# Paired score matmuls in a forgetting-attention mixer, and its convolution rows placed behind the weight splits on VectorE

## The chip, the cores and the metric

One core of a Trainium2 chip runs the whole program once. The time is device microseconds of one execution; smaller is better. Engines are called as in the profile: PE is TensorE's matmul side, PEld its weight load, DVE is VectorE, ACT is ScalarE, POOL is GpSimd, SP issues the DMAs.

## What is computed

A 256-token, 1024-wide float32 activation goes through three mixers and four feed-forward layers (FFN), in the order: differential attention with pooling, FFN 0, sliding-window attention, FFN 1, FFN 2, the forget mixer, FFN 3, final norm. The change matters in the forget mixer:

```
proj = rms_norm(x, mix_norm) @ w_in                 # a, g, q, k, v, fl
u = a * sigmoid(g)                                  # 512 channels
y = causal depthwise conv of u, 31 taps, + bias
y_conv = silu(layer_norm(y))
cum = cumsum(log_sigmoid(fl + forget_b))            # per head
s = q k^T / 8 + cum[query] - cum[key], causal       # 8 heads of 64, blocks of 128 queries
y_attn = softmax(s) v
x = x + concat(rms_norm(y_conv), rms_norm(y_attn)) @ w_out
```

The two attention mixers before it compute scores with the same helper.

## The kernel before, in words

**Tiling.** Tokens are two blocks of 128 (`tb` 0 and 1). Each weight matrix comes as tiles of 128 x 2048 float32 (1 MB). A tile is loaded by an SP DMA into one of two staging tiles `st`, then split in two: ACT casts it to the rounded part `whi` (two pieces of 128x1024, line 218) and DVE subtracts to get the rest `wlo` (four pieces of 128x512, line 222). `whi` and `wlo` have five buffers each. Each product is three matmuls, of lines 271, 272, 273 or 521, 522, 523: `whi` with the activation's rounded part, `wlo` with it, `whi` with the activation's rest. So PE needs both parts of a weight, a new cast needs the buffer of the fifth cast before it, and a new DMA needs a staging tile that has been read by ACT and DVE.

**Order.** The program is written in one order, and a scheduler in the build orders each engine's instructions by readiness and priority. Work under `tc.high_priority(offset=-N)` is set N places later in priority. The splits stand under `-LATER` (400) and the convolution's rows under `-LATERC` (300), so both give way to the work of the moment. Once built, each engine runs its own list in order and waits at an instruction whose input or buffer isn't ready.

**The forget mixer.** `conv_in(j)` projects 128 channels of a and g into `ag`; `cv[j].gate()` makes `u` from them (`th` on ACT, `u` on DVE). `conv_rows(cv[j])` adds the taps: each row is one DVE instruction over up to 256 tokens, `ys<-u,dwh,ys` (line 1090); tap 30 is the last, 226 tokens wide. One of the four channel blocks has 11 of its taps on PE (`cv`, line 1105). `proj_qk(s, b)` projects block b of q (s = 0) or k (s = 1) with 24 matmuls into `qk`; ACT copies it out. A block holds two heads, in partitions 0 to 63 and 64 to 127. `f0` and `f1` are the attention of the two query blocks; `scores(*blks)` calls `softmax_rows` (line 632: the q k product `sc<-qk,qk`, 64 rows deep, written in two passes and so two matmuls in the trace; lines 1158 and 1160: the gates' matmuls added into the same PSUM tile; line 635: DVE's reading of the tile, `S`, with the row minimum `nm`), then the exponentials on ACT. `ptp` and `o` are transposes and values; `on` (line 911) is the normed attention output, `z` (line 1178) its gated norm, `pt` the transposes of a `z`, and `mixT` the result, rounded part by ACT (line 289) and rest by DVE (line 290).

**The end of the mixer.** `conv_norm(tb)` transposes the convolution's `ys` on PE (`yT`, line 1192), takes mean and variance (BN_STATS), and goes through `yc`, `th` (ACT), `yc`, the square sum `junk` (ACT, line 299), `ss` (DVE), a power on POOL, `z`, `pt`, `mixT`. The output projection `op` has four weight tiles: two for the attention half of `mixT` (48 matmuls of 512 columns for both token blocks), two for the convolution half (48 more). Then come the residual, a norm and `lead`, the first matmuls of FFN 3.

Of the kernel before, what the change touches and what calls it, by code (L numbers as in the profile page):

```python
# [14 lines left out]
ALU = mybir.AluOpType  # L15
# [4 lines left out]
S = 256  # L20
# [8 lines left out]
SLOPES_A = [2.0 ** (-8.0 * (i + 1) / 4) for i in range(4)]  # L29
SLOPES_C = [float(np.float32(2.0) ** np.float32(-8.0 * (i + 1) / 16)) for i in range(16)]  # L30
# [5 lines left out]
FIRST = {("w0", 0): 4, ("w0", 1): 2}  # L36
TB, UB = 6, 5
NPE = (0, 11, 0, 0)
LATERC = 300
VCOPY = {((1, 0), 4), ((0, 0), 4), ((0, 1), 2), ((1, 1), 0), ((1, 1), 6)}  # L40
O_PS = {(1, 0), (1, 1)}
DENG = "AAAA"
# [67 lines left out]
def block_kernel(ctx: ExitStack, tc: tile.TileContext, a: dict, out: bass.AP):  # L110
    nc = tc.nc
    V, A, T, G = nc.vector, nc.scalar, nc.tensor, nc.gpsimd
# [12 lines left out]
    def ps_t(name="ps"):  # L125
        return pps.tile([P, 512], F32, tag="ps", name=name)

    def t512(name="t512"):
        return tmp.tile([P, 512], F32, tag="t512", name=name, bufs=TB)

    def b4(dt=F32, name="b4"):
        return tmp.tile([P, 1024], dt, tag="b4", name=name, bufs=5)
# [18 lines left out]
    def C(n, i=0, w=None):  # L151
        o, full = CC[n]
        return cc[:, o + i:o + i + (full - i if w is None else w)]
# [121 lines left out]
    def cut(pair, *idx):  # L275
        return tuple(t[idx] for t in pair)

    def tok(tb):
        return slice(tb * P, (tb + 1) * P)
# [98 lines left out]
    def v3(pair, k):  # L378
        return tuple(t.rearrange("p (k n) -> p k n", k=k) for t in pair)
# [139 lines left out]
    def mm_w(o, w, xT, ko, first, last):  # L519
        x = cut(xT, slice(None), ko, slice(0, S))  # L520
        T.matmul(o, w[0], x[0], start=first, stop=False)
        T.matmul(o, w[0], x[1], start=False, stop=False)
        T.matmul(o, w[1], x[0], start=False, stop=last)
# [56 lines left out]
    kTA = b4(name="kTA").rearrange("p (b t) -> p b t", b=4)  # L580
    qTA = b4(name="qTA").rearrange("p (b t) -> p b t", b=4)
# [38 lines left out]
        A.activation((qTA, kTA)[s][:, :, tok(tb)], transposes(hn.pop((s, tb)), 4).rearrange("p (b t) -> p b t", b=4),  # L620
                     AF.Copy, scale=(nqg, PVs("kg"))[s])

    def softmax_rows(qT, kT, heads, tb, rel, nm, den, SP, extra=None):

        L = P * (tb + 1)
        per = 512 // L
        for i in range(0, len(heads), per):
            pst = ps_t("sc")
            Sx = t512("S")
            for n, (r0, qb, kb, slope, idx) in enumerate(heads[i:i + per]):  # L630
                o = pst[:, n * L:(n + 1) * L]
                T.matmul(o, qT[r0:r0 + 64, qb, :], kT[r0:r0 + 64, kb, 0:L], start=True, stop=extra is None)  # L632
                if extra is not None:
                    extra(o, idx, L)
                V.tensor_tensor_reduce(Sx[:, n * L:(n + 1) * L], o, rel[:, S - L:S], slope, 3e38,
                                       ALU.add, ALU.min, nm[:, idx:idx + 1])
                SP[idx] = Sx[:, n * L:(n + 1) * L]

    def exps(idxs, SP, nm, den):
        for idx in idxs:  # L640
            A.activation(SP[idx], SP[idx], AF.Exp, bias=nm[:, idx:idx + 1], scale=-1.0,
                         accum_out=den[:, idx:idx + 1])

    class AttendA:
# [4 lines left out]

        def scores(self, *hs):  # L650
            tb, SP, rd, den = self.tb, self.SP, self.rd, self.den
            for m in range(2):
                softmax_rows(qTA[:, :, tok(tb)], kTA, [(64 * m, h, h, SLOPES_A[h], 2 * h + m) for h in hs],
                             tb, C("rel"), self.nm, den, SP)
            exps([2 * h + m for m in range(2) for h in hs], SP, self.nm, den)
            i = slice(2 * hs[0], 2 * hs[-1] + 2)
            V.reciprocal(rd[:, i], den[:, i])
            two = lambda t: t[:, i].rearrange("p (h m) -> p h m", m=2)
            ra = self.ra[:, hs[0]:hs[-1] + 1]
            V.scalar_tensor_tensor(ra, two(rd)[:, :, 1], nlam, two(den)[:, :, 0], ALU.mult, ALU.mult)  # L660
            for h in hs:
                p0, p1 = SP[2 * h], SP[2 * h + 1]
                V.scalar_tensor_tensor(p0, p1, self.ra[:, h:h + 1], p0, ALU.mult, ALU.add)
# [169 lines left out]
    qTC = [b4(name="qTC").rearrange("p (b t) -> p b t", b=4) for _ in range(2)]  # L833
# [81 lines left out]
    class AttendC(Values):  # L915
# [4 lines left out]
        def scores(self, *blks):  # L920
            c, tb, SP, nm, den, sk = self.c, self.tb, self.SP, self.nm, self.den, self.sk
            kT1 = kTC[c].rearrange("p (o t) -> p o t", o=1)
            for e in range(2):
                softmax_rows(qTC[c][:, :, tok(tb)], kT1,
                             [(64 * e, b, 0, SLOPES_C[8 * c + 2 * b + e], 2 * b + e) for b in blks],
                             tb, C("relw"), nm, den, SP)
            i = slice(2 * blks[0], 2 * blks[-1] + 2)
            V.tensor_tensor(nm[:, i], nm[:, i], nsink[:, 8 * c:8 * c + 8][:, i], ALU.min)
            exps([2 * b + e for e in range(2) for b in blks], SP, nm, den)
            V.tensor_tensor(sk[:, i], nm[:, i], srow[:, 8 + 8 * c:16 + 8 * c][:, i], ALU.add)  # L930
            A.activation(sk[:, i], sk[:, i], AF.Exp)
            V.tensor_tensor(den[:, i], den[:, i], sk[:, i], ALU.add)
            V.reciprocal(self.rd[:, i], den[:, i])
# [103 lines left out]
    for h in range(2):  # L1037
        hs = slice(h * 512, (h + 1) * 512)
# [17 lines left out]
    def conv_in(j):  # L1056
        ag[j] = ps_t("ag").rearrange("p (s t) -> p s t", s=2)
        w = v3(W.get("w2", j), KD)
        for s in range(2):
            for ko in range(KD):  # L1060
                mm_w(ag[j][:, s, :], cut(w, slice(None), ko, slice(s * P, (s + 1) * P)),
                     xT, ko, ko == 0, ko == KD - 1)
        W.free(("w2", j))
# [70 lines left out]
    def conv_rows(c):  # L1134
        with tc.high_priority(offset=-LATERC):
            c.rows()
# [4 lines left out]
    q2, k2 = (b4(name=f"qk{s}").rearrange("p (b t) -> p b t", b=4) for s in range(2))  # L1141

    def proj_qk(s, b):
        o = ps_t("qk")
        for ko in range(KD):
            mm_w(o[:, :S], cut(v3(W.get("w2", 4 + 2 * s + ko // 4), 4), slice(None), ko % 4, slice(b * P, (b + 1) * P)),
                 xT, ko, ko == 0, ko == KD - 1)
        A.activation((q2, k2)[s][:, b, :], o[:, :S], AF.Copy, scale=1.0 if s else -0.125)
        if b == 3:
            W.free(("w2", 4 + 2 * s), ("w2", 5 + 2 * s))  # L1150

    class AttendF(Values):
# [8 lines left out]
                         stop=kb == L // P - 1)  # L1161

        def scores(self, *blks):
            for e in range(2):
                softmax_rows(q2[:, :, tok(self.tb)], k2, [(64 * e, b, b, 1.0, 2 * b + e) for b in blks],
                             self.tb, C("mask"), self.nm, self.den, self.SP, self.gate)
            exps([2 * b + e for e in range(2) for b in blks], self.SP, self.nm, self.den)
            i = slice(2 * blks[0], 2 * blks[-1] + 2)
            V.reciprocal(self.rd[:, i], self.den[:, i])
# [37 lines left out]
    f0, f1 = AttendF(0), AttendF(1)  # L1207
    cv = [Conv(j, NPE[j]) for j in range(4)]
# [16 lines left out]
    proj_qk(0, 1)  # L1225
    conv_in(3)
    conv_rows(cv[2])
    proj_qk(1, 2)
    proj_qk(1, 1)
    proj_qk(0, 2)  # L1230
    proj_qk(1, 0)
    proj_qk(0, 3)
    cv[3].gate()
    f1.scores(0, 1)
    conv_rows(cv[3])
    f0.scores(0, 1)
    proj_qk(1, 3)
    f1.values_T(2, 3)
    f1.scores(2, 3)
# [133 lines left out]
```

## Time and profile before

| what | value |
| --- | --- |
| median of 3 runs | 1063.0 us |
| the runs shown | 1060.22, 1063.0, 4472.5 us |
| the profiled execution | 1060.59 us |
| its span in the trace | 1058.7 us |
| granted TensorE clock | 0.999 |
| PE, DVE, ACT busy | 1040.9, 779.4, 622.2 us |

The profiled execution is 1.9 us longer than its span and 2.4 us below the median of the runs shown. The forget mixer lies at about 745 to 865 us of the span. A busy share counts an engine as busy from the start to the modelled end of its instructions, so short steps in which matmuls follow each other slowly don't show as idle; there, the distance from one start to the next is what tells.

### The profile page before, as it was taken

To read this page: it belongs to the slowest core of one execution; us is meant where nothing else is said; L and a number is where in the kernel's file an instruction comes from. 1 tells how busy PE (TensorE), PEld (TensorE's weight loads), DVE (VectorE), ACT (ScalarE), POOL (GpSimd) and SP (SyncE) were. 2 spreads that over 40 slices of the span, in tenths; PEclk is the share of its full clock that TensorE was granted. 3 is DMA by queue.
4 is the path that set the end of the run, shared out by engine and by line. 5 is a ranking of instruction groups with operands and counts; after the bars stand their busy time and mean duration, and the time that the engine had idled before them with its cause. 6 is when DMAs were issued, how large, how long until landed. Compare 5 with 4: busy or idle time off the path is not lost.

```text
span 1058.7 us, 15504 instructions
## 1 busy us (share of the span) xinstructions
PE 1040.9 (98%) x5873; PEld 892.1 (84%) x5873; DVE 779.4 (74%) x1694; ACT 622.2 (59%) x1119; POOL 32.1 (3%) x40
## 2 busy tenths in 40 slices
PE   8999999999999999999999999999999999999997
PEld 5778988888877798888889888888898888888885
DVE  6686788878867578888787666656799896656662
ACT  6485666666657456666665555554644566554552
POOL 1100000000011000000000000000000010000000
PEclk9999999999999999999999999999999999999999
DMA  7635566655453074665545655554613156655531
GB/s 268 235 139 199 179 202 206 229 176 182 159 179 115 5 243 144 223 209 197 199 159 182 226 181 188 199 190 169 224 54 120 46 214 223 215 176 189 192 119 40
DMA packets 28746, 185.17 MB, mean 175 GB/s; under 512 B 3320, under 2 KB 4224, under 8 KB 7552
## 3 DMA queue, kind: packets, MB, share of 16 engines
q1 hardware_dynamic: 28672, 184.19, 50.0%
q8 instruction: 46, 0.75, 0.3%
q14 instruction: 28, 0.23, 0.1%
HBM read 183.13 MB, written 1.05 MB: 174 GB/s over the span
## 4 chain that ended last, share of the span: by engine, by line
PE 86%; DVE 6%; DMA 3%; ACT 2%; POOL 1%; issue 1%; SPq 0%; POOLq 0%; ACTq 0%; DVEq 0%
PE up L529 26%; PE up L531 14%; PE dn L271 7%; PE dn L272 7%; PE dn L273 7%; DVE wlo L222 2%; PE sc L632 2%; DMA st<-in_w 2%; PE proj L273 2%; PE o L896 2%; PE proj L272 1%; PE op L271 1%; PE op L273 1%; PE op L272 1%; PE lead L273 1%; PE lead L271 1%
## 5 line engine op out<-in xcount | busy, mean ns | idle before, releaser
L222 DVE TENSOR_TENSOR wlo<-st,whi 128x512 fp32r<-128x512 f32 x668 | 433.1, 686 | 158.2 <-ACT whi L218 158.1
L218 ACT CAST whi<-st 128x1024 fp32r<-128x1024 f32 (+1 forms) x336 | 339.1, 1042 | 131.1 <-PE dn L273 29.7
L529 PE MATMUL up<-xT,whi 128*128 128x512 f32 x1216 | 303.9, 392 | 0.8 <-DVE c L461 0.7
L529 PEld LDWEIGHTS up<-xT,whi 128*128 128x128 f32 x1216 | 220.7, 189 | 42.0 <-PE up L431 1.2
L531 PEld LDWEIGHTS up<-xT,wlo 128*128 128x128 f32 x1216 | 165.9, 190 | 11.9
L531 PE MATMUL up<-xT,wlo 128*128 128x256 f32 x1216 | 169.5, 282 | 0.0
L271 PE MATMUL dn<-whi,g 128*128 128x512 f32 x352 | 137.5, 391 | 0.0
L272 PE MATMUL dn<-wlo,g 128*128 128x512 f32 x352 | 137.1, 390 | 0.0
L273 PE MATMUL dn<-whi,g 128*128 128x512 f32 x352 | 136.7, 389 | 0.0
L536 ACT COPY h<-up 128x256 f32<-128x256 f32 x152 | 55.6, 366 | 69.3 <-PE up L531 69.0
L273 PEld LDWEIGHTS dn<-whi,g 128*128 128x128 f32 x352 | 66.1, 188 | 14.2 <-DVE g L473 0.3
L271 PEld LDWEIGHTS dn<-whi,g 128*128 128x128 f32 x352 | 66.2, 188 | 13.0 <-ACT g L472 0.4
L272 PEld LDWEIGHTS dn<-wlo,g 128*128 128x128 f32 x352 | 66.3, 188 | 12.2
L472 ACT CAST g<-m 128x256 fp32r<-128x256 f32 x88 | 35.6, 406 | 64.4 <-DVE m L468 64.4
L537 DVE TENSOR_TENSOR h<-up,h 128x256 f32<-128x256 f32 x152 | 63.6, 418 | 11.5 <-ACT h L536 11.4
L271 PE MATMUL lead<-whi,xT 128*128 128x256 f32 x192 | 55.6, 289 | 0.0
L273 PE MATMUL lead<-whi,xT 128*128 128x256 f32 x192 | 54.3, 283 | 0.0
L272 PE MATMUL lead<-wlo,xT 128*128 128x256 f32 x192 | 54.3, 283 | 0.0
L456 ACT ACTIVATE c<-h,pv 128x256 f32<-128x256 f32 x76 | 45.6, 602 | 6.1 <-DVE h L537 6.1
L473 DVE TENSOR_TENSOR g<-m,g 128x256 fp32r<-128x256 f32 x88 | 36.9, 422 | 16.5 <-ACT g L472 13.7
L272 PE MATMUL proj<-wlo,xT 128*128 128x512 f32 x112 | 44.9, 403 | 2.4 <-DVE wlo L222 2.3
L271 PE MATMUL proj<-whi,xT 128*128 128x512 f32 x112 | 44.6, 403 | 2.0 <-ACT whi L218 1.8
(227 smaller groups left out, 1366.4 us busy)
## 6 DMA issues: line engine op xcount, KB each, us to landing
st<-in_up SPq DMA_DIRECT2D x88, 1024.0 KB, 4.8
st<-in_dn SPq DMA_DIRECT2D x44, 1024.0 KB, 4.8
st<-in_w SPq DMA_DIRECT2D x21, 1024.0 KB, 4.8
gb<-in_rows SPq DMA_DIRECT2D x9, 512.0 KB, 4.2
st<-in_w0o SPq DMA_DIRECT2D x4, 1024.0 KB, 4.8
st<-in_w1o SPq DMA_DIRECT2D x4, 1024.0 KB, 4.7
st<-in_w2o SPq DMA_DIRECT2D x4, 1024.0 KB, 4.8
st<-in_w SPq DMA_DIRECT2D x4, 256.0 KB, 5.6
```

Of the source, the lines that this page charges most:

```text
L218: A.copy(hi[:, c], st[:, c])
L222: V.tensor_sub(lo[:, c], st[:, c], hi[:, c].bitcast(F32))
L271: T.matmul(o, l[0], r[0], start=first, stop=False)
L272: T.matmul(o, l[0], r[1], start=False, stop=False)
L273: T.matmul(o, l[1], r[0], start=False, stop=last)
L456: A.activation(cs[s], hs[s], AF.Identity, bias=PVs(cb, blk), scale=PVs(cw, 3 * blk + 2))
L472: A.copy(hi, m)
L473: V.tensor_sub(lo, m, hi.bitcast(F32))
L529: T.matmul(o, w[0], xT.both(ko), start=ko == 0, stop=False, skip_group_check=True)
L531: T.matmul(o[:, :S], w[1], xT[0][:, ko, :], start=False, stop=ko == KD - 1, skip_group_check=True)
L536: A.copy(h, o[:, S:])
L537: V.tensor_tensor(h, o[:, :S], h, ALU.add)
```

## The change

There are three edits. `softmax_rows` takes pairs of heads of one block and writes the two q k products, one from partitions 0 to 63 and one from 64 to 127, next to each other into two PSUM tiles; before, it went through the blocks for one half and then for the other, each product followed by its gates. `LATERC` goes from 300 to 700, so that the convolution's rows stand behind the splits (400). And the forget mixer's projections, scores and `conv_rows(cv[3])` are written in another order.

```diff
-LATERC = 300
+LATERC = 700
...
-    def softmax_rows(qT, kT, heads, tb, rel, nm, den, SP, extra=None):
+    def softmax_rows(qT, kT, pairs, tb, rel, nm, SP, extra=None):
+
         L = P * (tb + 1)
         per = 512 // L
-        for i in range(0, len(heads), per):
-            pst = ps_t("sc")
-            Sx = t512("S")
-            for n, (r0, qb, kb, slope, idx) in enumerate(heads[i:i + per]):
-                o = pst[:, n * L:(n + 1) * L]
-                T.matmul(o, qT[r0:r0 + 64, qb, :], kT[r0:r0 + 64, kb, 0:L], start=True, stop=extra is None)
-                if extra is not None:
-                    extra(o, idx, L)
-                V.tensor_tensor_reduce(Sx[:, n * L:(n + 1) * L], o, rel[:, S - L:S], slope, 3e38,
-                                       ALU.add, ALU.min, nm[:, idx:idx + 1])
-                SP[idx] = Sx[:, n * L:(n + 1) * L]
+        for i in range(0, len(pairs), per):
+            pst = [ps_t("sc") for _ in range(2)]
+            Sx = [t512("S") for _ in range(2)]
+            for n, pair in enumerate(pairs[i:i + per]):
+                at = slice(n * L, (n + 1) * L)
+                for e, (r0, qb, kb, slope, idx) in enumerate(pair):
+                    T.matmul(pst[e][:, at], qT[r0:r0 + 64, qb, :], kT[r0:r0 + 64, kb, 0:L], start=True,
+                             stop=extra is None)
+                for e, (r0, qb, kb, slope, idx) in enumerate(pair):
+                    o = pst[e][:, at]
+                    if extra is not None:
+                        extra(o, idx, L)
+                    V.tensor_tensor_reduce(Sx[e][:, at], o, rel[:, S - L:S], slope, 3e38,
+                                           ALU.add, ALU.min, nm[:, idx:idx + 1])
+                    SP[idx] = Sx[e][:, at]
...
-    proj_qk(1, 2)
-    proj_qk(1, 1)
-    proj_qk(0, 2)
-    proj_qk(1, 0)
-    proj_qk(0, 3)
-    cv[3].gate()
-    f1.scores(0, 1)
-    conv_rows(cv[3])
-    f0.scores(0, 1)
+    proj_qk(1, 1)
+    proj_qk(1, 0)
+    cv[3].gate()
+    f1.scores(0)
+    proj_qk(0, 2)
+    f1.scores(1)
+    conv_rows(cv[3])
+    proj_qk(1, 2)
+    f0.scores(0, 1)
+    proj_qk(0, 3)
     proj_qk(1, 3)
     f1.values_T(2, 3)
     f1.scores(2, 3)
```

The callers in the three mixers hand over the pairs in place of two lists. In the two earlier mixers the order of instructions stays as it was but for one swap of two rows on PE.

On PE, at the scores of blocks 2 and 3 for the second query block (`sc` is the PSUM tile of scores, the two tiles being the two halves), before and then after:

```order
L632 MATMUL sc_8224<-qk1_7417,qk0_7416 128x256
L1158 MATMUL sc_8224<-crow_7810,selr_7398 128x256
L1160 MATMUL sc_8224<-selr_7398,ncrow_7811 128x128 x2
L632 MATMUL sc_8236<-qk1_7417,qk0_7416 128x256
L1158 MATMUL sc_8236<-crow_7810,selr_7398 128x256
L1160 MATMUL sc_8236<-selr_7398,ncrow_7811 128x128 x2
```

```order
L634 MATMUL sc_8229<-qk1_7417,qk0_7416 128x256
L634 MATMUL sc_8230<-qk1_7417,qk0_7416 128x256
L1161 MATMUL sc_8229<-crow_7810,selr_7398 128x256
L1163 MATMUL sc_8229<-selr_7398,ncrow_7811 128x128 x2
L1161 MATMUL sc_8230<-crow_7810,selr_7398 128x256
L1163 MATMUL sc_8230<-selr_7398,ncrow_7811 128x128 x2
```

The two products that stood three rows apart now stand next to each other, in front of both gates.

On DVE, where the attention outputs `on` are normed, before and then after (`u_8084` and `u_7986` are the last channel block's `u`; its last row is the one with 226 tokens):

```order
L1090 SCALAR_TENSOR_TENSOR ys_7414<-u_8084,dwh_7396,ys_7414 128x227
L911 TENSOR_TENSOR on_8352<-o8_8343,rd_7420 128x512
L1090 SCALAR_TENSOR_TENSOR ys_7414<-u_8084,dwh_7396,ys_7414 128x226
L222 TENSOR_TENSOR wlo_8075<-st_7899,whi_8072 128x512
L911 TENSOR_TENSOR on_8363<-o8_8298,rd_7423 128x512
```

```order
L915 TENSOR_TENSOR on_8357<-o8_8348,rd_7420 128x512
L1093 SCALAR_TENSOR_TENSOR ys_7414<-u_7986,dwh_7396,ys_7414 128x241
L915 TENSOR_TENSOR on_8368<-o8_8303,rd_7423 128x512
L1177 TENSOR_SCALAR ss_8370<-ss_8370 128x1
L1093 SCALAR_TENSOR_TENSOR ys_7414<-u_7986,dwh_7396,ys_7414 128x240
L1180 SCALAR_TENSOR_TENSOR z_8376<-on_8357,rs_8374,gb_7394 128x512
```

Before, one row of the convolution was left when the first `on` came up; now 16 are left, and no piece of `wlo` stands between them.

On ACT, from the attention's `mixT` to the convolution's, before and then after (`whi` casts, `th` and `junk` of the convolution's norm, `pt_8467` and `pt_8472` the transposes of its first `z`):

```order
L289 ACTIVATE mixT_7413<-pt_8445 128x4x128
L218 CAST whi_8197<-st_8070 128x1024 x2
L1203 ACTIVATE th_8401<-yc_8391 128x512
L299 ACTIVATE junk_8405,ss_8404<-yc_8391 128x512
L289 ACTIVATE mixT_7413<-pt_8467 128x4x128
L218 CAST whi_8207<-st_8080 128x1024
```

```order
L289 ACTIVATE mixT_7413<-pt_8450 128x4x128
L218 CAST whi_8505<-st_8210 128x1024 x2
L1205 ACTIVATE th_8406<-yc_8396 128x512
L218 CAST whi_8560<-st_8220 128x1024 x2
L299 ACTIVATE junk_8410,ss_8409<-yc_8396 128x512
L289 ACTIVATE mixT_7413<-pt_8472 128x4x128
```

The casts here now belong to weight tiles two places further along the stream, and a pair of them has come to stand ahead of `junk`. `whi_8560` is the fifth tile after `whi_8156` (the second attention tile of the output projection) and takes its buffer.

## Rows read from the trace of the kernel before

**Rows 1.** The page: PE's busy time, and the chain by engine.

```profile
PE 1040.9 (98%) x5873; PEld 892.1 (84%) x5873; DVE 779.4 (74%) x1694; ACT 622.2 (59%) x1119; POOL 32.1 (3%) x40
...
PE 86%; DVE 6%; DMA 3%; ACT 2%; POOL 1%; issue 1%; SPq 0%; POOLq 0%; ACTq 0%; DVEq 0%
```

**Rows 2.** Busy time by stretch: stretch, its length, then each engine.

```profile
795.00:830.00 35.00, 35.00 (x235) 29.69 (x234) 33.13 (x104) 19.05 (x50) 0.00 (x0) 1.00 0.26 91
830.00:845.00 15.00, 14.02 (x93) 12.12 (x94) 12.78 (x29) 8.52 (x21) 2.34 (x3) 1.00 0.21 71
```

**Rows 3.** Waits of PE, 745 to 892 us: total, times, longest.

```profile
PE qk L523 <- DVE wlo L222: 1.2, 3, 0.5
PE pt L543 <- DVE z L1178: 0.6, 1, 0.6
PE up L431 <- ACT lead L422: 0.4, 1, 0.4
```

**Rows 4.** Timeline of PE in the forget mixer: start, us, instruction.

```profile
807.60 0.70 PE L632 MATMUL sc<-qk,qk 64*128 64x256 f32 x2
808.22 0.39 PE L1158 MATMUL sc<-crow,selr 128*128 128x256 f32 x1
...
815.33 0.48 PE L632 MATMUL sc<-qk,qk 64*128 64x128 f32 x2
```

**Rows 5.** Timeline of PE in the two earlier mixers: products next to each other.

```profile
50.80 0.49 PE L632 MATMUL sc<-kTA,qTA 64*128 64x128 f32 x4
...
322.16 1.04 PE L632 MATMUL sc<-kvC,qTC 64*128 64x256 f32 x4
...
323.72 0.70 PE L632 MATMUL sc<-kvC,qTC 64*128 64x256 f32 x4
```

**Rows 6.** Timeline of DVE: splits, convolution rows, and the first `on`.

```profile
802.49 0.68 DVE L222 TENSOR_TENSOR wlo<-st,whi 128x512 fp32r<-128x512 f32 x1
803.09 0.47 DVE L1090 SCALAR_TENSOR_TENSOR ys<-u,dwh,ys 128x250 f32<-128x250 f32 x1
803.48 0.69 DVE L222 TENSOR_TENSOR wlo<-st,whi 128x512 fp32r<-128x512 f32 x1
...
833.98 0.69 DVE L911 TENSOR_TENSOR on<-o,rd 128x512 f32<-128x512 f32 x1 [0.55 <-PE o L896]
834.59 0.45 DVE L1090 SCALAR_TENSOR_TENSOR ys<-u,dwh,ys 128x226 f32<-128x226 f32 x1
```

**Rows 7.** Waits of DVE, 764 to 866 us.

```profile
DVE S L635 <- PE sc L1160: 1.1, 4, 0.4
DVE S L635 <- PE cv L1105: 0.9, 1, 0.9
```

**Rows 8.** Timelines of ACT and DVE: the convolution's norm, first token block.

```profile
842.36 2.00 ACT L218 CAST whi<-st 128x1024 fp32r<-128x1024 f32 x2
...
846.61 0.63 ACT L299 ACTIVATE junk<-yc 128x512 bf16<-128x512 f32 x1 [1.17 <-DVE yc L1204]
847.15 0.18 ACT L299 ACTIVATION_READ_ACCUMULATOR junk<-yc 128x1 f32 x1
...
847.63 0.15 DVE L1175 TENSOR_SCALAR ss<-ss 128x1 f32<-128x1 f32 x1
...
848.82 0.75 DVE L1178 SCALAR_TENSOR_TENSOR z<-yc,rs,gb 128x512 f32<-128x512 f32 x1 [0.44 <-POOL rs L294]
```

**Rows 9.** Timeline of PE: output projection and the start of FFN 3.

```profile
840.17 0.50 PE L271 MATMUL op<-whi,mixT 128*128 128x512 f32 x1
...
849.50 0.39 PE L273 MATMUL op<-whi,mixT 128*128 128x512 f32 x1
849.73 0.63 PE L543 MATMUL pt<-cc,z 128*128 128x128 f32 x4
...
850.87 0.67 PE L271 MATMUL op<-whi,mixT 128*128 128x512 f32 x2
...
865.38 0.28 PE L271 MATMUL lead<-whi,xT 128*128 128x256 f32 x1
```

More of the change, by code (lines that the diff above doesn't have):

```diff
@@ L651, in scores @@
             tb, SP, rd, den = self.tb, self.SP, self.rd, self.den
-            for m in range(2):
-                softmax_rows(qTA[:, :, tok(tb)], kTA, [(64 * m, h, h, SLOPES_A[h], 2 * h + m) for h in hs],
-                             tb, C("rel"), self.nm, den, SP)
+            softmax_rows(qTA[:, :, tok(tb)], kTA, [[(64 * m, h, h, SLOPES_A[h], 2 * h + m) for m in range(2)] for h in hs],
+                         tb, C("rel"), self.nm, SP)
             exps([2 * h + m for m in range(2) for h in hs], SP, self.nm, den)
@@ L922, in scores @@
             kT1 = kTC[c].rearrange("p (o t) -> p o t", o=1)
[L923 to L926, printed above, removed]
+            softmax_rows(qTC[c][:, :, tok(tb)], kT1,
+                         [[(64 * e, b, 0, SLOPES_C[8 * c + 2 * b + e], 2 * b + e) for e in range(2)] for b in blks],
+                         tb, C("relw"), nm, SP)
             i = slice(2 * blks[0], 2 * blks[-1] + 2)
@@ L1163, in scores @@
         def scores(self, *blks):
-            for e in range(2):
-                softmax_rows(q2[:, :, tok(self.tb)], k2, [(64 * e, b, b, 1.0, 2 * b + e) for b in blks],
-                             self.tb, C("mask"), self.nm, self.den, self.SP, self.gate)
+            softmax_rows(q2[:, :, tok(self.tb)], k2, [[(64 * e, b, b, 1.0, 2 * b + e) for e in range(2)] for b in blks],
+                         self.tb, C("mask"), self.nm, self.SP, self.gate)
             exps([2 * b + e for e in range(2) for b in blks], self.SP, self.nm, self.den)
```

## The prediction

> **What bounds the kernel now.** I read the page first. PE is busy for 98% of the span and 86% of the chain of work that ended last is PE's [rows 1], so a saved microsecond counts when it is PE's, and a lost one when PE has nothing else to run. The change touches only the forget mixer, so I went to its stretch. There the table by stretch shows a second full engine: between 795 and 830 us DVE works for 33.13 of 35 us while PE reads as full [rows 2]. PE's list of waits in the mixer is short: 1.2 us for `wlo`, 0.6 us for a `z`, 0.4 us for a `lead` [rows 3]. DVE in turn waits for PE's scores, 1.1 and 0.9 us [rows 7]. The reader is to see two engines that run nearly neck and neck, DVE full with the convolution's rows, which are its filler, and no cover to spare at the end of the mixer: the convolution's first `z` is transposed at 849.73 and only four matmuls of other work stand behind that before the convolution half of the output projection begins [rows 9].
>
> **The pairs.** The mixer has sixteen products, eight 256 wide and eight 128 wide. A single 256-wide product takes 0.62 us to the next start (807.60 to 808.22) [rows 4]. In the earlier mixers two products from the two halves are already next to each other: four matmuls take 0.70 us busy, as two do alone, in one row, and 1.04 us, 0.34 more, in another [rows 5]. So a pair saves between 0.28 and 0.62 us. For 128 columns it is 0.48 us for two and 0.49 for four [rows 4, 5]; busy is some 0.08 us longer than the distance of starts, so a pair saves 0.40. In the new order all four 256-wide pairs stand together, of the 128-wide ones two do. At most that is 4 x 0.62 + 2 x 0.40 = 3.3 us, at least 4 x 0.28 + 2 x 0.40 = 1.9. I take 3.3, since the products stand before gates here as in the faster row.
>
> **The `wlo` that come sooner.** With the rows behind the splits, the rests of the two k tiles stand right behind the second `u` on DVE, some 20 us ahead of where they were. The 1.2 us of PE's wait for them goes [rows 3]. What is late next: the first scores now stand directly behind the projection of k's block 0, and PE must wait for ACT to copy that out. No row shows it; the nearest is the transposes of a `z`, a copy by ACT and the matmul that reads it, 1.4 us with 0.45 us of transposes in it (below), so up to 0.95; the other end is nothing. I take 0.7. With the 0.6 us wait for `z` gone as well, PE would be 3.3 + 1.2 + 0.6 - 0.7 = 4.4 us early at the output projection, at 835.8 in place of 840.17 [rows 9].
>
> **What DVE makes of it.** A piece of `wlo` takes 0.60 us (802.49 to 803.09), a row of the convolution 0.39 [rows 6]. I counted DVE's order from the second `u` on. Ahead of the first `on` now stand 28 pieces where 15 stood, 13 x 0.60 = 7.8 us more, and 15 rows of the convolution fewer, 15 x 0.39 = 5.9 us. So DVE comes to `on` 1.9 us later by its own work. It had waited 0.55 us there for PE [rows 6] and 2.0 us for scores on the way [rows 7]. If all of these waits go, `on` starts at 833.98 - 0.55 - 2.0 + 1.9 = 833.3; if those for scores stay, at 835.3. In the old trace the first `op` starts 6.2 us after `on` (840.17 against 833.98) [rows 6, 9]; of this I take off 1.2 for two pieces of `wlo` that stood between. So `op` starts between 838.3 and 841.5. I take 839.5. Of PE's 4.4 us, 0.7 are left: the scores wait for DVE, which is where the eight pieces in a row of the last two output tiles now stand, just ahead of the scores of blocks 2 and 3.
>
> [...]
>
> **The last rows of the convolution.** They ended at 834.95 (834.59 and 0.36) [rows 6]. By DVE's order 13 pieces (7.8 us), a second `on`, two `z` and two rests of `mixT` (five of some 0.6, 3.1 us) and small ones (0.5) now come before: 834.95 + 11.4 = 846.4. PE hides this behind the attention half of the output projection, 48 matmuls of 0.23 us (849.50 to 849.73) [rows 9]; the transposes `yT` that need the last row stand behind the 31st of them, at about 839.5 + 31 x 0.23 + 0.5 = 847.1. So this is just covered, with 0.7 us to spare; each microsecond beyond costs one.
>
> **The gap behind the attention half.** In the old order, the first matmul of the convolution half is the second of the two at 850.87, so at about 851.1; from 840.17 there are 10.9 us with 40 of the 48 attention matmuls. Now all 48 come before the transposes of the convolution's `z`: 839.5 + 10.9 + 8 x 0.23 - 0.45 (those transposes) + 0.2 (two of `yT`) = 852.0 is when the last ends. Behind it PE has no other work in its order, and what it needs isn't begun: on ACT the two casts of `whi_8560` stand ahead of `junk`, and they need the buffer that this last attention matmul frees. So after 852.0 come, one after the other: casts 2.0, `junk` with its read 0.72 (846.61 to 847.33), from `ss` to the start of `z` 1.19, from there to `pt` 0.91 (848.82 to 849.73) [rows 8, 9], from `pt` to the first matmul of the convolution half 1.4 (849.73 to 851.1) [rows 9], and two handings over between engines that I estimate at 0.1 each: 6.4 us. The other branch, over DVE, ends a little sooner: BN_STATS can begin at about 847.3, and in the old trace 8.0 us lay between it and `z`, so `z` at 855.3 against 856.1 by the casts. The convolution half starts at 858.4.
>
> In the old trace it is 865.38 - 851.1 = 14.3 us from there to `lead` [rows 9], with eight attention matmuls (1.8) in it that are done by now: 12.5. The second `z`'s transposes and copy (1.4, of which 0.45 transposes) had attention matmuls to hide behind and have none now: 0.9 more. `lead` starts at 858.4 + 13.4 = 871.8, 6.4 us late. FFN 3 keeps PE full, so this passes to the end, less the 0.4 us wait for `lead` copies [rows 3], since weights are further ahead. GpSimd's order is the same; SP's loads come 5 to 15 us sooner at the end of the mixer, in a stretch where DMA is busy for 0.21 of the time [rows 2].
>
> **Sum.** -0.7 (earlier `op`) + 7.1 (6.4 + 0.9 + 0.2 - 0.45 and rounding) - 0.4 = +6.0 us. Against the profiled execution of 1060.6 us that is 1066.6. The median of the runs shown is 2.4 us above the profiled one; I stay with 1066.6.
>
> **Rivals.** First, *not slower*: DVE isn't what holds `on`. Then `op` starts at 835.8 as PE alone would have it, 3.7 us before my 839.5, and the second gap closes (0.9) because DVE is ahead by as much: 1066.6 - 4.6 = 1062.0, no slower than the median shown. It decides at `on` starting by 831 (835.8 - 5.0). For it: DVE's waits for PE were 2.5 us. Against it: `on` needs 2.3 us more than all these waits give (833.3). Second, *the convolution's last row ends later than 847*: PE then stands at `yT` in the middle of the projection, and every microsecond is one more. DVE now waits for POOL's power at both `z` of the attention with rows behind them, where pieces of `wlo` had stood, and ACT's casts for the last output tiles are released only by the last q projection. With 3.5 us of such waits it is 850.5, and 1070. Third, *the pairs don't run side by side*: 1.9 in place of 3.3 us saved, of which DVE hides most; with `op` at 840.2 it gives 1067.3.
>
> **How the numbers follow.** The forecast of 1066.6 has a chance of 0.5, the first rival 0.2, the second 0.2, the third 0.1. Ends: `op` at 835.8, no second gap and the two casts not in the way (2.0) would give 1066.6 - 3.7 - 0.9 - 2.0 = 1060.0; `op` at 841.5 and a last row 2 us beyond its cover give 1070.6. As runs of the kernel before differ by 2 us at the low end too, the range is 1058 to 1071. About 2%, 21 us, is what a measurement of this kernel can tell from no change; no case comes near it, so I give 0.97 to within 2%, 0.01 to faster and 0.02 to slower.
>
> **What would show it.** In the new trace: singles of 0.62 replaced by four matmuls in 0.70; no wait of `qk` for `wlo`; the first `op` within a microsecond of 840; the convolution's 226-wide row at about 846; a wait of PE for `pt<-z` of about 5 us near 852 and one of about 1 us for `mixT` behind it and behind the second; `lead` at about 872. If `lead` starts before 867 the gap was mis-sized, and I am wrong in the casts' place; if PE waits at `yT`, the second rival is right; if the `op` starts at 836, the first.

## The result, and the profile after

The median of the kernel after is 1070.05 us (20 runs, 1068.37 to 1073.21) against 1061.66 of the kernel before (20 runs): a ratio of 1.0079 [1.0069, 1.0089], 8.4 us more. One run of the kernel before took 4472.5 us; it is in that median, but not in the ratio. The profiled execution took 1069.72 us, with a span of 1067.8 us and a granted clock of 0.996 over the whole program. The forecast was 1066.6 us.

The page's line on PE shows nothing of this: it is as busy as before [rows 1].

```profile
PE 1041.2 (98%) x5873; PEld 892.8 (84%) x5873; DVE 781.7 (73%) x1695; ACT 622.1 (58%) x1119; POOL 31.2 (3%) x40
```

The list of PE's waits from 745 to 900 us does (total, times, longest). Of the three waits in [rows 3], those for `wlo` and for `lead` are gone and the one for `z` has doubled to 1.3 us; a wait of 5.3 us in front of a `pt` is new. The list puts it down to `mv` on DVE. What PE waits for is `z`, as the DVE rows further down show.

```profile
PE pt L543 <- DVE mv L1199: 5.3, 1, 5.3
PE sc L634 <- DVE nm L640: 1.9, 2, 1.5
PE op L271 <- ACT mixT L289: 1.4, 2, 0.7
PE pt L543 <- DVE z L1180: 1.3, 1, 1.3
PE qk L521 <- DVE u L1081: 1.1, 1, 1.1
PE sc L634 <- ACT qk L1151: 0.5, 1, 0.5
```

PE's timeline of after, first where the scores of pairs of 256-wide products are made (against [rows 4]), then the output projection up to FFN 3 (against [rows 9]):

```profile
797.00 0.70 PE L634 MATMUL sc<-qk,qk 64*128 64x256 f32 x4 [0.47 <-ACT qk L1151]
797.63 0.39 PE L1161 MATMUL sc<-crow,selr 128*128 128x256 f32 x1
...
798.19 0.33 PE L1163 MATMUL sc<-selr,ncrow 128*128 128x128 f32 x2
798.36 0.33 PE L521 MATMUL qk<-xT,whi 128*128 128x256 f32 x1
...
801.37 0.86 PE L634 MATMUL sc<-qk,qk 64*128 64x256 f32 x4
...
820.08 1.04 PE L634 MATMUL sc<-qk,qk 64*128 64x256 f32 x4 [0.39 <-DVE nm L640]
...
839.72 0.50 PE L271 MATMUL op<-whi,mixT 128*128 128x512 f32 x1
...
847.20 0.39 PE L271 MATMUL op<-whi,mixT 128*128 128x512 f32 x1
847.72 0.44 PE L1194 MATMUL yT<-cc,ys 128*128 128x128 f32 x2
...
851.67 0.39 PE L273 MATMUL op<-whi,mixT 128*128 128x512 f32 x1
857.41 1.09 PE L543 MATMUL pt<-cc,z 128*128 128x128 f32 x4 [5.35 <-DVE mv L1199]
859.18 0.79 PE L271 MATMUL op<-whi,mixT 128*128 128x512 f32 x1 [0.69 <-ACT mixT L289]
...
860.20 0.63 PE L271 MATMUL op<-whi,mixT 128*128 128x512 f32 x1
860.63 0.63 PE L273 MATMUL op<-whi,mixT 128*128 128x512 f32 x1
...
874.88 0.28 PE L271 MATMUL lead<-whi,xT 128*128 128x256 f32 x1
```

The first `op` comes 0.45 us earlier than before, the first `lead` 9.5 us later. All of the loss lies between these two rows: 35.16 us in place of 25.21. Within it, PE stands from 851.9 (the last start and 0.23 us) to 857.41, and that is the gap the prediction spoke of. But look at the distance of starts behind it: 860.20 to 860.63 is 0.43 us for one matmul of 512 columns, where 849.50 to 849.73 was 0.23 before [rows 9]. The table of stretches (length, PE, PEld, DVE, ACT, POOL busy, PEclk, DMA share, GB/s) tells why:

```profile
856.00:858.00 2.00, 0.59 (x3) 0.62 (x4) 1.56 (x6) 0.00 (x0) 0.48 (x1) 0.85 0.89 373
858.00:860.00 2.00, 1.31 (x5) 0.82 (x4) 1.90 (x3) 1.06 (x2) 0.55 (x1) 0.50 0.75 172
860.00:862.00 2.00, 2.00 (x6) 1.52 (x6) 0.96 (x3) 0.90 (x3) 0.08 (x1) 0.50 1.01 430
862.00:864.00 2.00, 2.00 (x6) 1.56 (x5) 0.75 (x1) 0.00 (x0) 0.47 (x1) 0.50 0.73 270
864.00:866.00 2.00, 2.00 (x10) 1.60 (x9) 0.05 (x1) 0.00 (x0) 0.00 (x0) 0.95 0.00 0
```

From 857.4 to 864.2 us the granted clock is half, 0.50 in each stretch from 858 to 864, directly after PE stood for 5.35 us by the profile. PE reads as fully busy there (2.00 of 2.00) and does less: 6 matmuls in 2 us, where 10 follow.

What PE waits for is seen on ACT and DVE (against [rows 8]). ACT's timeline from the attention's `mixT` on:

```profile
849.35 2.00 ACT L218 CAST whi<-st 128x1024 fp32r<-128x1024 f32 x2 [7.73 <-PE op L273]
851.89 0.63 ACT L1205 ACTIVATE th<-yc 128x512 f32<-128x512 f32 x1 [0.53 <-DVE yc L1203]
852.42 1.98 ACT L218 CAST whi<-st 128x1024 fp32r<-128x1024 f32 x2
854.30 0.62 ACT L299 ACTIVATE junk<-yc 128x512 bf16<-128x512 f32 x1
```

And DVE's, from the first `on` (against [rows 6]) to the convolution's first `z`:

```profile
834.33 0.69 DVE L915 TENSOR_TENSOR on<-o,rd 128x512 f32<-128x512 f32 x1 [1.34 <-PE o L900]
...
842.26 5.40 DVE L1093 SCALAR_TENSOR_TENSOR ys<-u,dwh,ys 128x236 f32<-128x236 f32 x11
848.08 1.30 DVE L1198 BATCH_NORM_STATS2 st<-yT 128x6 f32<-128x512 f32 x2 [0.42 <-PE yT L1194]
...
853.52 1.89 DVE L222 TENSOR_TENSOR wlo<-st,whi 128x512 fp32r<-128x512 f32 x3
855.33 0.14 DVE L1177 TENSOR_SCALAR ss<-ss 128x1 f32<-128x1 f32 x1
...
856.51 0.75 DVE L1180 SCALAR_TENSOR_TENSOR z<-yc,rs,gb 128x512 f32<-128x512 f32 x1 [0.44 <-POOL rs L294]
```

The convolution's last eleven rows, which had been done by 835 [rows 6], run from 842.26 to 847.66. Then follows the convolution's norm. On ACT the second pair of casts stands between its `th` and its `junk`, on DVE pieces of `wlo` stand between its steps, and PE has nothing else in its order.

### The profile page after: what moved, and what is told of

It reads as the page before. It is cut to its first block, busy times and chain, and to the rows that moved or that the text cites. A ratio compares the mean times of both kernels' runs of the same rounds, so it can differ in the third digit from the quotient of the medians.

```text
span 1067.8 us, 15511 instructions
## 1 busy us (share of the span) xinstructions
PE 1041.2 (98%) x5873; PEld 892.8 (84%) x5873; DVE 781.7 (73%) x1695; ACT 622.1 (58%) x1119; POOL 31.2 (3%) x40
## 4 chain that ended last, share of the span: by engine, by line
PE 88%; DVE 7%; ACT 2%; DMA 2%; POOL 1%; issue 1%; POOLq 0%; ACTq 0%; SPq 0%
PE up L529 26%; PE up L531 14%; PE dn L271 7%; PE dn L272 7%; PE dn L273 7%; PE lead L271 2%; PE lead L273 2%; PE lead L272 2%; DVE ys L1093 2%; PE op L271 2%; DVE wlo L222 2%; PE op L273 2%; PE op L272 2%; DMA st<-in_w 2%; PE sc L634 2%; PE o L900 1%
## 5 line engine op out<-in xcount | busy, mean ns | idle before, releaser
L473 DVE TENSOR_TENSOR g<-m,g 128x256 fp32r<-128x256 f32 x88 | 37.0, 423 | 16.5 <-ACT g L472 13.7
L299 ACT ACTIVATE junk<-x 128x512 bf16<-128x512 f32 x32 | 20.2, 630 | 45.5 <-DVE x L365 26.9
```

What stands on the lines that cost most here:

```text
L473: V.tensor_sub(lo, m, hi.bitcast(F32))
```

## The experiments

The theory: the rows' place in DVE's order makes the loss, by a gap on PE that the written order and the pairs neither make nor mend; and behind the gap the lower clock adds some 3 us. The rivals: the new written order by itself makes the gap; the pairs disturb something; or the gap's size comes from the casts in front of `junk`.

In the table, the ratio is to the runs of the kernel before taken beside that kernel, so it need not be the quotient of two medians here. `op` and `lead` are the first of each in the profiled execution. "Rows" counts the convolution's rows that stand behind the first `on` in DVE's order. The clock is the mean over a kernel's runs of the granted clock of the whole program. For the kernel before, the clock is that of its 64 runs above 0.990 beside all of these kernels.

| kernel | median us (runs) | ratio to before | `op` | `op` to `lead` | rows | clock |
| --- | --- | --- | --- | --- | --- | --- |
| before | 1061.66 (20) | 1 | 840.17 | 25.21 | 1 | 0.9960 |
| after | 1070.05 (20) | 1.0079 [1.0069, 1.0089] | 839.72 | 35.16 | 16 | 0.9934 |
| e1_rows300 | 1060.73 (12) | 0.9973 [0.9949, 0.9997] | 843.77 | 24.61 | 3 | 0.9975 |
| e2_rows700_alone | 1076.54 (5) | 1.0142 [1.0117, 1.0168] | 847.16 | 33.91 | 15 | 0.9868 |
| e3_pairs_alone | 1061.1 (11) | 0.9981 [0.9958, 1.0004] | 839.63 | 25.26 | 3 | 0.9976 |
| e4_order_alone | 1061.4 (11) | 0.9985 [0.9966, 1.0005] | 841.82 | 25.09 | 1 | 0.9981 |
| e5_pairs_700 | 1071.82 (5) | 1.0091 [1.0064, 1.0118] | 840.83 | 35.45 | 18 | 0.9912 |
| e6_warm | 1069.3 (6) | 1.006 [1.004, 1.008] | 845.65 | 32.47 | 16 | 0.9958 |
| e7_casts_behind | 1069.07 (6) | 1.0054 [1.0036, 1.0072] | 842.11 | 33.14 | 16 | 0.9942 |
| e8_two_blocks | 1061.54 (12) | 0.9997 [0.9984, 1.001] | 841.59 | 24.88 | 0 | 0.9961 |
| e9_rows450 | 1062.93 (12) | 1.0008 [0.9995, 1.0021] | 843.06 | 25.29 | 3 | 0.9958 |
| e10_rows450_split | 1065.8 (12) | 1.0031 [1.0019, 1.0043] | 843.03 | 29.74 | 9 | 0.9939 |

**The rows put back, the rest kept (e1_rows300).**

```diff
-LATERC = 700
+LATERC = 300
```

> The changed kernel with the convolution's rows back at 300, ahead of the splits; pairs and the new written order stay. Theory (the rows' place alone opens the gap at the output projection, and the half clock follows from that gap): 19 pieces of wlo instead of 28 stand ahead of the last row, the gap goes, PE keeps some of the 3 us that the pairs save, and the time is 1058 to 1062, against 1061.7 before and 1070.0 after. Rival (the new order with its waits of PE for PSUM and score readings is what costs): 1066 or more.

The median is 1060.73 us, and `lead` follows `op` by 24.61 us. PE's timeline shows `pt` of the convolution's `z` without a wait, at 852.09 between attention matmuls:

```profile
843.77 0.47 PE L271 MATMUL op<-whi,mixT 128*128 128x512 f32 x1
...
852.09 0.63 PE L543 MATMUL pt<-cc,z 128*128 128x128 f32 x4
...
868.38 0.28 PE L271 MATMUL lead<-whi,xT 128*128 128x256 f32 x1
```

So the loss goes with the one number. The `op` itself came late in this profile, and the stretches show why: the clock was half from 822.6 to 829.4 us. PE had waited for score tiles (`sc` for `nm`) ahead of it, 0.8 us up to 810.4 and 0.6 us up to 819.8:

```profile
820.00:824.00 4.00, 4.00 (x23) 3.26 (x23) 3.78 (x14) 2.78 (x10) 0.00 (x0) 0.83 0.01 2
824.00:828.00 4.00, 4.00 (x14) 3.63 (x14) 3.28 (x8) 2.18 (x8) 0.00 (x0) 0.50 0.00 0
```

This profiled execution, at 1063.03 us, is the second slowest of its twelve. The wait for `wlo`, 1.2 us, is back with the rows.

**The rows alone (e2_rows700_alone)**, in the kernel before:

```diff
-LATERC = 300
+LATERC = 700
```

> The kernel before with nothing changed but the rows' place, 700 for 300. Theory (the rows' place): 28 pieces ahead of the last row as after the whole change, a gap of about 6 us behind the attention half of the output projection, a low clock behind it, 1067 to 1071. Rival (pairs and new order cost): within 2 us of 1061.7.

This is the slowest kernel of all. The gap is there without pairs and in the old written order. In PE's timeline and in the stretches:

```profile
863.56 0.63 PE L543 MATMUL pt<-cc,z 128*128 128x128 f32 x4 [4.10 <-DVE mv L1197]
...
881.07 0.28 PE L271 MATMUL lead<-whi,xT 128*128 128x256 f32 x1
```

```profile
862.00:866.00 4.00, 1.75 (x7) 1.35 (x8) 3.50 (x8) 0.71 (x2) 1.18 (x2) 0.77 0.78 262
866.00:870.00 4.00, 4.00 (x11) 3.13 (x10) 2.40 (x5) 1.35 (x3) 0.55 (x1) 0.50 0.66 190
```

A second loss is in the score stage. In the old order a PE wait of 1.7 us for `nm` was followed by half clock from 809 to 823 us, and `op` started 7 us later than before. So the pairs and the new order do help under 700 (1.0142 against 1.0079), but only against a harm that 700 itself makes.

**The pairs alone (e3_pairs_alone)** and **the written order alone (e4_order_alone)**, both at 300. In e3, seen from after:

```diff
-LATERC = 700
+LATERC = 300
...
+    proj_qk(1, 2)
     proj_qk(1, 1)
+    proj_qk(0, 2)
     proj_qk(1, 0)
+    proj_qk(0, 3)
     cv[3].gate()
-    f1.scores(0)
-    proj_qk(0, 2)
-    f1.scores(1)
+    f1.scores(0, 1)
     conv_rows(cv[3])
-    proj_qk(1, 2)
     f0.scores(0, 1)
-    proj_qk(0, 3)
```

In e4, the new order of these lines was put into before.

> The kernel before with the pairs alone: old written order, the convolution's rows at 300. Theory (pairs save PE up to 3.3 us, and as no more work stands ahead of the convolution's last row than about 19 pieces, no gap opens): 1 to 3 us below the kernel before. Rival (VectorE, full there, takes all of it): no difference.

> The kernel before with the new written order alone: single products, rows at 300. Theory (the order by itself neither opens the gap nor saves PE time, and adds a wait of 0.5 us for a copy of k): 0 to 1 us above the kernel before. Rival (the order is what costs the 8 us): 5 us above or more.

Neither interval lies clear of no change. All scores are written in pairs in e3, but the scheduler set some apart again: in the trace two of the four 256-wide pairs and one of the four 128-wide ones run side by side. So e3 tests part of the pairs' saving. Here is PE's part of the table of stretches (length, PE busy, PEclk, DMA share, GB/s). The first two rows are the matmuls of `sc` alone, before and after; for e3 it is 13.51 us. The other three are all of PE's work from the first `qk` matmul to the first `op`, before, after and in e3:

```profile
790.00:833.00 43.00, 15.67 (x72) 1.00 0.21 74
790.00:833.00 43.00, 12.27 (x72) 1.00 0.23 78
776.74:840.17 63.43, 61.59 (x445) 1.00 0.17 57
776.36:839.72 63.36, 57.93 (x442) 1.00 0.33 116
776.29:839.63 63.34, 60.17 (x444) 1.00 0.24 84
```

In this stretch PE is busy for 3.7 us less in after and 1.4 less in e3, and the stretch is as long as before. What PE saves is lost again in waiting, most of it for DVE, as the prediction took it. The first `op` of e3 is 0.54 us sooner than before, but 0.45 of this lies ahead of the first `qk`. The order alone gives PE the wait of 0.5 us for the copy of k's block 0. In the profile of e4 `op` came 1.65 us later than before, with half clock from 793.7 to 797.1 us.

**The pairs and 700, old written order (e5_pairs_700)**, seen from after:

```diff
+    proj_qk(1, 2)
     proj_qk(1, 1)
+    proj_qk(0, 2)
     proj_qk(1, 0)
+    proj_qk(0, 3)
...
-    f1.scores(0)
-    proj_qk(0, 2)
-    f1.scores(1)
+    f1.scores(0, 1)
...
-    proj_qk(1, 2)
     f0.scores(0, 1)
-    proj_qk(0, 3)
```

> The changed kernel with the old written order: pairs and rows at 700. Theory (rows at 700 open the gap in either order): 7 to 12 us above the kernel before, with a wait of PE of some 5 us ahead of the transposes of the convolution's first z and a half clock behind it. Rival (the gap comes from the new order): within 3 us of the kernel before.

It has the same stretch as after, 35.45 us, with a wait of 6.72 us in front of the `pt`. With e2 this settles that at 700 the gap doesn't come from the written order.

**PE kept at work in the gap (e6_warm).** Twenty matmuls of 512 columns, whose result is overwritten, stand in front of the transposes of the convolution's first `z`; these follow as they were, and nothing else is changed.

```diff
     def mix_T(blk, tb):
+        if (blk, tb) == (0, 0):
+            pt, z = ps_t("pt"), zs.pop((blk, tb))
+            with tc.high_priority(offset=-5000):
+                for i in range(20):
+                    T.matmul(pt, mixT[0][:, 7, tok(1)], xT[0][:, 0:2, :], start=True, stop=True)
...
```

> The changed kernel with 20 matmuls more, of 512 columns and with no use, which write the PSUM tile of the convolution's first transposes before these and so stand in the gap; all else stays in its place, and no work is left out. Theory (the fall of the granted clock behind the gap costs some 3 us by itself: 12 matmuls took 0.43 in place of 0.23 us, four transposes and a first matmul 0.7 more): the clock stays at 1.0, lead starts 3 us sooner, 1067. Rival (the matmuls behind the gap are slow for another reason, or the fillers cost as much as they save): 1070.

The `pt` still starts 17.59 us behind `op` (863.24 - 845.65; in after 857.41 - 839.72 = 17.69): the gap is as long, only filled. The clock stays at 1.00 behind it, and from there to `lead` it is 14.88 us in place of 17.47. So the lower clock behind the gap cost 2.6 us. PE's timeline and the stretches:

```profile
863.24 0.66 PE L1195 MATMUL pt<-cc,z 128*128 128x128 f32 x4 [0.74 <-DVE z L1180]
...
878.12 0.28 PE L271 MATMUL lead<-whi,xT 128*128 128x256 f32 x1
```

```profile
862.00:866.00 4.00, 2.58 (x13) 1.70 (x12) 3.48 (x7) 0.66 (x2) 0.94 (x2) 1.00 0.79 281
866.00:870.00 4.00, 4.00 (x20) 3.30 (x19) 1.94 (x4) 1.30 (x3) 0.55 (x1) 1.00 0.86 340
```

The median fell by 0.75 us only, less than the two intervals can tell apart. In the profiled execution `op` came 5.9 us later than in after. Of this, 3.05 us lie ahead of the first `qk` (779.41 against 776.36), where half clock from 35 to 39 us, near the start of the program, is seen in this trace alone. The rest goes with half clock from 806.6 to 813.4 us, around a PE wait of 2.6 us for `nm`. Why this execution had them, with an edit behind both, is open.

**The casts behind the convolution's norm (e7_casts_behind).** Two columns of that `z` are copied into the buffers of the next two weight tiles before these are cast, so that the casts can't stand ahead of `junk`.

```diff
+                if key in (("up3", 1), ("up3", 2)):
+                    V.tensor_copy(hi[:, ::CH // 2], zs0[0][:, 0:2])
...
+    zs0 = []
...
+        zs0.append(zs[0, tb])
```

> The changed kernel with the splits of FFN 3's second and third weight tiles held until the convolution's first z is there (a copy of two of its columns into the cast's buffer), so that neither their casts nor their pieces of wlo stand in the convolution's norm. Theory of the prediction (casts ahead of the square sum set the gap, the DVE branch ends 0.8 us sooner): z comes 0.8 to 1.7 us sooner, 1068 to 1069.5. Rival (the chain from the convolution's last row sets it whatever ACT does): 1070. Should the shorter gap keep the clock up, 1066.

```profile
857.55 0.81 PE L546 MATMUL pt<-cc,z 128*128 128x128 f32 x4 [3.12 <-DVE mv L1203]
...
875.25 0.28 PE L274 MATMUL lead<-whi,xT 128*128 128x256 f32 x1
```

From `op` to `pt` it is now 15.44 us, 2.25 less, and the wait fell from 5.35 to 3.12. The last row ends 7.93 us behind `op` in both, so the whole difference lies in the norm. So casts and their `wlo` pieces were worth 2.2 us of the gap; the rest is the norm's own chain behind the last row. This is more than the 0.8 to 1.7 of the theory. The median, 1069.07 us, lies in its range, though the intervals of e7 and after overlap. The clock fell behind this shorter gap as well (a mean of 0.77 from 860 to 870 us; 17.70 us from `pt` to `lead`).

**Fewer rows late (e8_two_blocks, e9_rows450, e10_rows450_split).** In e8 only the rows of `cv[0]` and `cv[1]` stand at 700; in e9 all stand at 450; e10 is e9 with two projections and scores put in another order.

```diff
-        with tc.high_priority(offset=-LATERC):
+        with tc.high_priority(offset=-(LATERC if c.j in (0, 1) else 300)):
```

```diff
-LATERC = 700
+LATERC = 450
```

```diff
-    proj_qk(1, 1)
     proj_qk(1, 0)
+    proj_qk(1, 1)
...
-    f0.scores(0, 1)
+    f0.scores(0)
     proj_qk(0, 3)
+    f0.scores(1)
```

> The changed kernel with the rows of the first two channel blocks at 700 and those of the last two at 300. The rests of the k tiles stay early, as at 700, but only 18 pieces stand ahead of the last row, which now comes ahead of the attention's norms. Theory (the early rests save PE's 1.2 us wait, the late rows cost the gap, and the two can be had apart): no gap, no wait of qk for wlo, 3 to 5 us below the kernel before, 1057 to 1059. Rival (the new waits of PE for score readings eat it): as the kernel before or up to 2 us above.

> The changed kernel with 450 in place of 700 for the convolution's rows, nothing else. In DVE's order the rests of the k tiles stay where they are at 700, but only 20 pieces stand ahead of the last row, and 3 rows behind the first on. Theory (what costs is the splits of the output and FFN tiles ahead of the rows, not the early rests): the distance from the first op to lead is 25 us as before, not 35, and the time is 1057 to 1061. If PE's waits for score readings are followed by a half clock as in the versions at 300, it is at the upper end; rival (rows behind splits cost at any value): 1066 or more.

> The version at 450 with the written order changed at two places: k's block 0 is projected ahead of block 1, so that the first scores don't wait for a copy that has just begun, and the two scores of the first query block stand on either side of the projection of q's block 3, so that the second pair doesn't wait for DVE to read the first. Theory (waits of PE of 0.5 to 2.6 us in the score stage, and the half clock that followed them in five of the seven traces at 300 or 700, cost 2 to 5 us): no such wait, granted clock 1.0 throughout the score stage, 1056 to 1059, below the kernel before. Rival (VectorE holds the attention's norm whatever PE does): as the version at 450.

All three were to come out ahead of before, and none did. In e8 and e9 the gap is closed (24.88 and 25.29 us) and the wait for `wlo` gone, but `op` starts 1.4 and 2.9 us later. In e8 a PE wait of 1.2 us for `nm` ends at 809.68, and the stretches show half clock behind it, as in e1:

```profile
808.00:812.00 4.00, 2.82 (x15) 2.30 (x16) 3.91 (x17) 1.79 (x7) 0.00 (x0) 0.93 0.00 0
812.00:816.00 4.00, 4.00 (x25) 4.00 (x24) 4.00 (x13) 2.65 (x6) 0.00 (x0) 0.64 0.02 4
```

Nine rows behind `on` in e10 give a wait of 1.9 us for the `pt`, half clock behind it (0.50 from 860 to 862 us), and 29.74 us. Only the written order differs between e9 and e10, so at 450 the order does decide how many rows are left behind `on`, 3 or 9, and by that whether there is a gap. With the table's other kernels this orders itself: 0 to 3 rows give 24.6 to 25.3 us, 9 give 29.7, 15 to 18 give 33.9 to 35.5 with the clock down.

## Why the prediction came out as it did

The mechanism of the loss and the sign were right, and the 0.8% lies within the 2% that had a chance of 0.97. The size was 3.1 us short of the profiled execution's own rise: +6.0 forecast, 1069.72 - 1060.59 = +9.1 seen.

- **Pairs.** The saving was sized right: PE's busy time on `sc` is 3.4 us less (15.67 and 12.27), 3.3 were forecast. It is made up in another way. Two of the four 256-wide pairs run in 0.70 us as forecast, and one with its gates takes 1.36 us (797.00 to 798.36). A single took 1.11 before (807.60 [rows 4] to the next product at 808.71), so this pair saves 0.86, not 0.62, because the four gates behind each other are quicker as well. For 128 columns it is 2 x 0.78 (810.14 to 810.92) less 0.92 (807.26 to 808.18), 0.64 in place of 0.40. But the other two 256-wide pairs take 0.86 and 1.04 us (801.37 and 820.08), as the second product starts 0.17 and 0.34 us behind the first (801.54 and 820.42), where it is 0.01 in the quick ones. So the third rival is half true, and the quicker gates make up for it.
- **`wlo` sooner.** The wait is gone. In its place are 0.5 us for ACT's copy of `qk` (taken: 0.7) and two that weren't in the prediction, 1.1 us for `u` and 1.9 for `nm`, both on DVE's work. The wait for `z`, which was to go, grew from 0.6 to 1.3 us.
- **The first `on`.** It starts at 834.33, between the 833.3 and 835.3 given, and `op` at 839.72 (839.5 given). So the first rival, by which `op` would come at 835.8, is out, and e3 says the same from the other side. But the reason given for the time of `on`, DVE's own work, doesn't hold at the last step: DVE stood idle for 1.34 us in front of `on`, waiting for PE's `o`, where that wait was to go. DVE had held PE up earlier, by the waits for `u` and `nm`. That `on` came out within 1 us is in part luck, and so is the 0.45 us at `op`, of which 0.38 lie ahead of the first `qk` (776.36 against 776.74). So of the 4.4 us by which PE was to be early nearly nothing was left, 0.07. The waits that took it were only in part for the reading of score tiles, 1.9 us.
- **Last rows.** They end at 847.66, 1.3 us later than the 846.4 given. The cover had 0.7 us. PE reached `yT` at about 847.4 (847.20 + 0.23) and started it at 847.72, so the second rival came true by some 0.3 us, but not by the waits for POOL that it named: they are 0.44 us each, as before. The last eleven rows add to one `ys`, each to what the row just before wrote, and take 5.40 us, 0.49 each. At the 0.39 that the forecast gave a row they would take 4.3; that is 1.1 of the 1.3 us.
- **Gap.** The last attention matmul ends at 851.9 (852.0 given), `ss` and `z` start at 855.33 and 856.51 (856.1 for `z`), `pt` at 857.41 (857.0), with the casts ahead of `junk` as read from the order. They start at 852.42, not when the last attention matmul frees their buffer but when `th`, which stands ahead of them and waits for DVE's `yc`, has ended; that is the 0.4 us. The casts' part was undersized: 0.8 us between the two branches, 2.2 by e7. The 8.0 us taken for the branch over DVE had five pieces of `wlo` in it; in e7, without pieces, it is 6.2 from BN_STATS (850.46) to `z` (856.66). That changes nothing in the sum, since the chain through the casts was the one summed. The 0.1 us for a handing over had no row beside it; in the trace of before `yc` ends at 846.52 and `junk`, which waits for it, starts at 846.61.
- **From `pt` to `lead`.** This is the term that was mis-sized: 871.8 - 857.0 = 14.8 us given, 17.47 seen. It was priced from the row of 0.23 us for a matmul, and no term stood for the granted clock, which was half after the standstill of 5 us. In e6, with the clock up, the same stretch is 14.88.
- **To the end.** From `lead` on it is 192.92 us against 193.32 before, the 0.4 us gain that was forecast.

With the chain of times: -0.45 at `op`, +9.95 to `lead`, -0.40 behind it, +9.1 in all; of the 9.95, 2.6 are the clock's by e6.

The runs, each with its mean clock, say it in another way, which the profile of a single execution can't. Over 170 runs of all kernels here but e2 (those with a mean clock above 0.990), each 0.001 less of mean clock goes with 0.78 us more in the runs of the same kernel. Brought to the same clock by that slope, the mean of after stands 5.8 us above that of before (with five runs more at a clock of 0.986 to 0.988, the slope is 0.89 and the difference 5.4), near the 6.0 forecast. The other 2.0 us are the mean clock, 0.9934 in place of 0.9960. The 6.8 us at half clock behind the gap are 0.003 of the program, about what lies between the two. These are runs that vary by themselves, so the slope shows that the two go together, and only e6 shows the cause, for one place.

What stays open is the score stage. PE waits there for DVE's reading of score tiles in nearly all of these kernels. Behind or around such waits, 1.2 to 3.0 us in all, the profiles of e1, e2, e5, e6, e7, e8 and e9 show half clock for 3.4 to 13.7 us. That of after shows none behind 1.5 us. In e10 half clock came from 821 to 828 us with waits of no more than 0.8 in the stage, and in e4 from 793.7 to 797.1 with none above 0.5. In e8 and e9 it lasts for 3.4 us in the stage, which costs 1.6 us at most (an estimate: 3.4 less 3.4 x 0.23 / 0.43). In e8 3 to 5 us were hoped for, so this isn't all that was missing. No kernel here tells what decides it.

The best kernel is e1, pairs and new order with the rows where they were: 0.9973 [0.9949, 0.9997] of before, just clear of no change, and some 1% below after. The intervals of e3 and e4 overlap with its own, and two of the seventeen runs of before beside it had a mean clock of 0.986; without these two the quotient of the means is 0.9986 in place of 0.9975. That e1 is faster than before isn't shown.

## What to carry to other kernels

Work that fills an engine's idle time may be put off only until its last consumer needs it: before filler is moved behind something, find the last row of it in the engine's order, and what other work its consumer has left to hide the chain that follows. A standstill of TensorE may cost more than itself: here 6.8 us at half clock followed 5.35 us of waiting and cost 2.6 more, which the busy share didn't show; so read the distance of starts and the granted clock behind each wait. Taking work from one of two engines that run neck and neck gave nothing here, however well the saving itself came out. And whether a wait set a time is read from the row: a forecast time that comes true doesn't show that the reason given for it did.

## What the runs showed of the hardware

The granted clock is half (0.50) behind single waits of PE of 1.9 to 6.7 us at the end of the mixer in every profile that has one (after, e2, e5, e7, e10), and in several behind shorter ones, in the score stage and, in e9, right at the first `op` (842.3 to 845.8 us, behind waits of 1.6 and 0.5). One 512-column matmul is 0.43 us from start to start then, 0.23 otherwise. It differs by execution: the mean clock of after's 20 runs goes from 0.991 to 0.996.

Gate matmuls of 128 rows right behind a 64-row product took 0.49 us for one product's (808.22 to 808.71), and 0.73 for those of two products in a row (797.63 to 798.36), 0.25 less than twice 0.49. I had not expected a saving there.

A row of the convolution on DVE starts 0.39 us after the row before it where the rows of two `ys` take turns (six from 807.48 to 809.79 in after), and 0.49 where it adds to the `ys` that the row just before wrote (eleven from 842.26 to 847.66).
